# A hybrid decoder trunk on one core: the two merge gates as seven-product blocks, the attention projection behind them, and another order of the block products

## The chip, the cores and the metric

The kernel runs on one core of one Trainium2 chip. The metric is the device time of one execution in microseconds (us), lower is better. Before the change it is 2224.86 us (median of 3 runs, 2223.46 to 2225.05).

## The reference, cut to what matters

Two layers, 512 tokens, width 1024, all in float32. Each layer has a token-mixing sublayer and a SwiGLU sublayer, and the residual stream is normalized after each.

```python
z = einsum('bsd,dc->bsc', x, w_in) + b_in          # one projection, 11648 columns
q_a, k_a, v_a, q_r, k_r, v_r, g_r, gate_a, gate_b = split(z)
y_a = dilated_window_attention(q_a, k_a, v_a)      # 3 groups combined, width 384
y_b = silu(g_r) * group_norm(retention(q_r, k_r, v_r))   # 4 heads, width 2048
merged = sigmoid(gate_a) * (y_a @ w_attn_proj) + sigmoid(gate_b) * (y_b @ w_ret_proj)
x = layer_norm(ALPHA * x + merged @ w_out)
h = silu(x @ w_gate) * (x @ w_up)                  # D_FF = 2816
x = layer_norm(ALPHA * x + h @ w_down)
```

`gate_a` and `gate_b` are the last two pieces of the input projection, 1024 columns each. They read the layer's input `x`, the same for both.

## The kernel before, in words

**Numbers in two parts.** Each float32 operand is held as a high part (rounded to the matmul's float32r format) and a low part, the rest. `hilo` makes them: a copy on ACT for the high part, a subtraction on DVE for the low one. A product takes three matmuls: high x high, high x low, low x high (`mm3`, line 83; all of them appear in the profile as L81). `unit` (line 112) does the same for a tile of weights, which `load` (line 107) brought by a DMA of SP's queue into one of eight buffers of the pool `rawp`. The parts lie in `whi` and `wlo`, four buffers each.

**Tiles.** A tile of PSUM is 128 x 512, and there are eight. The layer's input lies transposed in `xh` and `xl`: 128 partitions by 8 pieces of the width by 512 tokens.

**Plain products.** `wstat` takes 128 columns of weights as the stationary operand and all 512 tokens as the moving one, 8 x 3 matmuls of 512.

**Block products.** Where two halves of the width, two halves of the tokens and two halves of the columns meet, the kernel multiplies 2 x 2 blocks with seven products instead of eight (Winograd's form). The left blocks are A11, A12, A22 (parts of `xh`, `xl`) and four sums S1 to S4 of blocks, which `x_sums` has put into `xs`; the right blocks are weights: B11, B21, B22, and sums P1 to P4. P1 and P3 are made by DMA: SP loads one block and a DMA of POOL's queue adds the second one to it in place (`Right.load`, L314). P2 and P4 are made from P1 in place by a DVE addition (`Right.begin`, L340). `Right.high` makes the high part (L323) and, one step later, the low part (L329); the operands of a product are prepared one product ahead (`Right.operands`). The table `ORDER` says in which order the products go, and `CHAIN` which PSUM tile a product adds to: products 1, 6, 7 and 4 add to tile A, 5 and 3 to tile C, 2 has its own:

```python
ORDER = ((1, "A11", "B11"), (2, "A12", "B21"), (5, "S1", "P1"), (3, "S4", "B22"),
         (6, "S2", "P2"), (7, "S3", "P3"), (4, "A22", "P4"))
CHAIN = {1: "A", 6: "A", 7: "A", 4: "A", 2: "X", 5: "C", 3: "C"}
```

After each product, `ev` reads what the tile holds by then: a copy on ACT after 1, 5 and 6, an addition or subtraction on DVE after 2, 3 and 7, the rest after 4. `wide` (line 390) runs such a block with 256 columns of weights stationary and 256 tokens moving: 7 x 24 matmuls of 256 columns. Before the change only the FFN uses it, in `ffn_pair`: 256 columns of the up matrix and the same 256 of the gate matrix, ten such pairs a layer (in parts of 2, 4 and 4, each followed by its share of the down projection). `tall` is the other form, with tokens stationary; it serves the values and gates of the retention heads (`ret_values_gates`) and the attention's values, and follows `ORDER` too.

**Order of the work.** The text gives an order, and the framework's scheduler then orders the instructions of each engine by its own estimate of what is ready, so that matmuls of a later product can stand ahead of an earlier one. Besides, the kernel keeps a list `side` of small steps (attention blocks, retention scores and outputs, transposes), which `tick` takes one by one between matmuls at a rate that `pace` sets; `drain` runs what is left.

**The stage that changes.** At the end of the mixing sublayer, after the last retention head's values and gates, a loop runs over four passes `dp` of 256 output channels. A pass computes both gates with `wstat` (4 x 24 matmuls of 512), takes the sigmoid (L916), stores gate b to the DRAM tile `g_d` by a DMA of ACT's queue (L918), loads 256 columns of `w_attn_proj`, multiplies them with the attention output `ya` (18 matmuls of 512), multiplies that by gate a (L928) and stores it to `g_d` by a DMA of POOL's queue (L929). In `side` meanwhile: the outputs of head 3 (`ret_outputs(3)`), then the first half of the retention output `y_d`, which is loaded (`y_load`) and split into `xs` (`y_put`), since nobody needs the sums in there any more. The next stage reads `g_d` back, and multiplies `w_ret_proj` with the retention output; it puts the second half of it into `xh` and `xl`.

Of the kernel before, what the change touches and what calls it, by code (L numbers as in the profile page):

```python
# [11 lines left out]
F32 = mybir.dt.float32  # L12
F32R = mybir.dt.float32r
AF = mybir.ActivationFunctionType
ALU = mybir.AluOpType
# [3 lines left out]
P = 128  # L19
S = 512  # L20
D = 1024
KD = D // P
# [4 lines left out]
NG = 3  # L27
# [14 lines left out]
C_GA = C_GR + RH * RV  # L42
C_GB = C_GA + D
# [10 lines left out]
def hybrid_kernel(ctx, tc, x, rel_bias, w_in, b_in, w_attn_proj, w_ret_proj, w_out,  # L54
# [3 lines left out]
    pe, act, dve, pool = nc.tensor, nc.scalar, nc.vector, nc.gpsimd  # L58
# [32 lines left out]
    def hilo(src, hi, lo):  # L91
        act.copy(out=hi, in_=src)  # L92
        dve.tensor_tensor(out=lo, in0=src, in1=hi.bitcast(F32), op=ALU.subtract)  # L93
# [4 lines left out]
    def work(name):  # L98
        return wk.tile([P, S], F32, tag="w2", name=name)
# [7 lines left out]
    def load(src, a, b):  # L107
        v = view(raw(), a, b)
        nc.sync.dma_start(v, src)
        return v  # L110

    def unit(v):
        a, b = v.shape[1], v.shape[2]
        h = view(wp.tile([P, 1024], F32R, tag="whi", name="whi"), a, b)
        l = view(wp.tile([P, 1024], F32R, tag="wlo", name="wlo"), a, b)
        hilo(v, h, l)
        return h, l
# [13 lines left out]
    side, rate, credit, awaited = deque(), [1.0], [0.0], [0] * NI  # L131
# [9 lines left out]
    def pace(us):  # L141
        rate[0], credit[0] = len(side) / us, 0.0

    def drain():
        while side:
            side.popleft()()
# [49 lines left out]
    def pair_units(w, c, c2=None):  # L196

        vs = []
        for hf in range(2):
            ks = slice(4 * hf, 4 * hf + 4)  # L200
            if c2 is None:
                vs.append(load(w[:, ks, c:c + 256], 4, 256))
            else:
                vs.append(view(raw(), 4, 256))
                for q, cc in enumerate((c, c2)):
                    nc.sync.dma_start(vs[hf][:, :, q * P:(q + 1) * P], w[:, ks, cc:cc + P])
        return [unit(v) for v in vs]
# [20 lines left out]
    def wstat(us, q):  # L228

        need(*range(NI))  # L230
        ps = psum("ps")
        for k in range(KD):
            h, l = part_of(us, k, q)
            mm3(ps, h, l, xh[:, k], xl[:, k], k == 0, k == KD - 1)
            tick(STEP)
        return ps
# [41 lines left out]
    def tail_units(raws):  # L278

        out_ = []  # L280
        for j, r in enumerate(raws):
# [12 lines left out]
    ORDER = ((1, "A11", "B11"), (2, "A12", "B21"), (5, "S1", "P1"), (3, "S4", "B22"),  # L294
             (6, "S2", "P2"), (7, "S3", "P3"), (4, "A22", "P4"))
    CHAIN = {1: "A", 6: "A", 7: "A", 4: "A", 2: "X", 5: "C", 3: "C"}
    FIRST = (1, 2, 5)

    class Right:

        def __init__(self, src, shapes):
            self.src, self.shapes, self.t = src, shapes, {}

        def load(self, *names):
            for n in names:
# [24 lines left out]
        def begin(self, n):  # L333

            if n == "B11":
                self.load("B11", "B21", "P1", "P3", "B22")
            elif n in ("P2", "P4"):
                for u in range(len(self.shapes)):
                    r = self.t["P1", u]
                    dve.tensor_tensor(out=r, in0=r, in1=self.t["B22" if n == "P2" else "B21", u], op=ALU.add)  # L340
            return self.high(n)

        def operands(self):

            ahead = self.begin("B11")
            for i in range(len(ORDER)):
                now, low = ahead
                low()
                ahead = self.begin(ORDER[i + 1][2]) if i + 1 < len(ORDER) else None
                yield now  # L350

    def x_left(an, j, ts_):

# [35 lines left out]

    def wide(right, left, ev):  # L390

        ps = {}
        for (i, an, bn), ((h, l),) in zip(ORDER, right.operands()):
            c = CHAIN[i]
            if i in FIRST:
                ps[c] = psum("ps")
            for q in range(2):
                cs = slice(q * P, (q + 1) * P)
                for k in range(4):
                    ah, al = left(an, k, slice(0, 256))  # L400
                    mm3(ps[c][:, q * 256:(q + 1) * 256], h[:, k, cs], l[:, k, cs], ah, al,
                        i in FIRST and q == 0 and k == 0, k == 3)
                    tick(STEP / 2)
            if i != 3:
                ev(i, ps[c])
            if i == 6:
                ev(3, ps["C"])
            yield

    def run(g):  # L410
        for _ in g:
            pass
# [204 lines left out]
    def layer(ly, cp):  # L617
        w_l = rows(w_in[ly])
# [3 lines left out]
        def bcol(c):  # L622
            return bT[:, c // P:c // P + 1]
# [10 lines left out]
        def slot(name="op", dt=F32R):  # L634
            return opp.tile([P, 2, S], dt, tag="op", name=name)
# [179 lines left out]
        with stage("ret") as rp:  # L815
# [64 lines left out]
                side.extend(ret_outputs(h))  # L880


            ya = []
            for t in range(NG):
                o_ = slot("ya")
                hilo(yaT[:, t], o_[:, 0], o_[:, 1])
                ya.append(o_)
            wa_l, wr_l = rows(w_attn_proj[ly]), rows(w_ret_proj[ly])
            y_v = rows(y_d)
            ylow = xs.rearrange("p s h k t -> p (s h k t)").rearrange("p (h k t) -> p h k t", h=2, k=KD)  # L890
# [2 lines left out]
            def y_load(q):  # L893
                yraw[q] = load(y_v[:, 2 * q:2 * q + 2], 2, S)
# [4 lines left out]
            def y_put(q):  # L899
                if q < 4:  # L900
                    hilo(yraw[q], ylow[:, 0, 2 * q:2 * q + 2], ylow[:, 1, 2 * q:2 * q + 2])
                else:
                    ks = slice(2 * q - KD, 2 * q - KD + 2)
                    hilo(yraw[q], xh[:, ks], xl[:, ks])

            for q in range(4):
                side.extend([lambda q=q: y_load(q)] + [nothing] * 4 + [lambda q=q: y_put(q)])
            pace(80)
            for dp in range(KD // 2):
                sg = []  # L910
                for b, c in enumerate((C_GA, C_GB)):
                    us = pair_units(w_l, c + dp * 256)
                    t = slot("sg", F32)
                    for e in range(2):
                        ps = wstat(us, e)
                        act.activation(out=t[:, e], in_=ps, func=AF.Sigmoid, bias=bcol(c + (2 * dp + e) * P))  # L916
                    sg.append(t)
                act.dma_start(g_d[1, dp * 256:(dp + 1) * 256].rearrange("(e p) s -> p e s", p=P), sg[1])  # L918
                h, l = unit(load(wa_l[:, :, dp * 256:(dp + 1) * 256], NG, 256))
                if dp == KD // 2 - 1:  # L920
                    drain()
                for e in range(2):
                    cs = slice(e * P, (e + 1) * P)
                    ps = psum("ps")
                    for t in range(NG):
                        mm3(ps, h[:, t, cs], l[:, t, cs], ya[t][:, 0], ya[t][:, 1], t == 0, t == NG - 1)
                    v = sg[0][:, e]
                    dve.tensor_tensor(out=v, in0=v, in1=ps, op=ALU.mult)  # L928
                pool.dma_start(g_d[0, dp * 256:(dp + 1) * 256].rearrange("(e p) s -> p e s", p=P), sg[0])  # L929
        lay.close()  # L930

        fin = ExitStack()
# [101 lines left out]

        def ffn_pair(f, o_):

            def src(b, u):
                k = 4 if b[1] == "2" else 0
                return (wg_l if b[2] == "2" else wu_l)[:, k:k + 4, f * P:f * P + 256]

            sn = {}

            def put(v, ts_):
                hilo(v, o_[:, 0, :, ts_], o_[:, 1, :, ts_])

            def ev(i, ps):
                p2 = ps.rearrange("p (q t) -> p q t", q=2)
                if i in (1, 5, 6):
                    sn[i] = work("sn").rearrange("p (q t) -> p q t", q=2)
                    act.copy(out=sn[i], in_=p2)  # L1050
                elif i == 2:
                    dve.tensor_tensor(out=sn[1], in0=p2, in1=sn[1], op=ALU.add)
                elif i == 3:
                    v = sn[6]
                    dve.tensor_tensor(out=v, in0=p2, in1=v, op=ALU.subtract)
                    act.activation(out=v, in_=v, func=AF.Silu)
                    dve.tensor_tensor(out=v, in0=v, in1=sn[1], op=ALU.mult)
                    put(v, slice(0, 256))
                elif i == 7:
                    dve.tensor_tensor(out=sn[5], in0=sn[5], in1=p2, op=ALU.subtract)  # L1060
                    act.activation(out=sn[5], in_=sn[5], func=AF.Silu)
                elif i == 4:
                    v = sn[5]
                    dve.tensor_tensor(out=v, in0=v, in1=p2, op=ALU.mult)
                    put(v, slice(256, 512))

            run(wide(Right(src, [(4, 256)]), x_left, ev))

        for part, (f0, f1) in enumerate(FPARTS):
            ht = []  # L1070
# [89 lines left out]
```

## Time and profile before

| | |
|---|---|
| median of 3 runs | 2224.86 us |
| the profiled execution | 2224.68 us |
| its span | 2222.9 us |
| granted TensorE clock | 0.998 |
| PE busy | 2184.1 us (98%), 12330 matmuls |
| DVE busy | 1352.1 us (61%) |
| ACT busy | 946.8 us (43%) |
| POOL busy | 233.5 us (11%) |
| DMA | 325.92 MB, mean 147 GB/s |

The span runs from the first to the last instruction that was profiled. PE is TensorE's matmul, PEld its weight load, DVE the vector engine, ACT the scalar engine, POOL GpSimd, SP the engine that only issues DMAs here; a q behind a name means the engine's queue of DMA issues. In the views, `out<-in` names the tiles that an instruction writes and reads, L81 is line 81 of the kernel, and a bracket at the end of a timeline row tells the idle time of the engine before it and what ended it. A row of a windows view has the window, its length, and the busy time and count of PE, PEld, DVE, ACT and POOL, then the granted clock, the DMA share and GB/s. A row of a group has busy time and mean ns of one, then the idle time before.

### The profile page before, as it was taken

To read this page: it belongs to the slowest core of one execution; us is meant where nothing else is said; L and a number is where in the kernel's file an instruction comes from. 1 tells how busy PE (TensorE), PEld (TensorE's weight loads), DVE (VectorE), ACT (ScalarE), POOL (GpSimd) and SP (SyncE) were. 2 spreads that over 40 slices of the span, in tenths; PEclk is the share of its full clock that TensorE was granted. 3 is DMA by queue.
4 is the path that set the end of the run, shared out by engine and by line. 5 is a ranking of instruction groups with operands and counts; after the bars stand their busy time and mean duration, and the time that the engine had idled before them with its cause. 6 is when DMAs were issued, how large, how long until landed. Compare 5 with 4: busy or idle time off the path is not lost.

```text
span 2222.9 us, 31189 instructions
## 1 busy us (share of the span) xinstructions
PE 2184.1 (98%) x12330; PEld 1884.7 (85%) x12330; DVE 1352.1 (61%) x1971; ACT 946.8 (43%) x1517; POOL 233.5 (11%) x280
## 2 busy tenths in 40 slices
PE   8999999999999999999999999999999999999998
PEld 7877788888888898989898778888888889899896
DVE  5643677875245675646676447777843357666575
ACT  4444544545333253525245445444543234444350
POOL 3110011100000100000040100111000001010001
PEclk9999999999999999999999999999999999999999
DMA  8944266455656356556269343666455562565551
GB/s 226 238 124 103 63 157 170 132 141 157 207 179 190 85 144 141 161 133 152 86 160 243 105 94 85 151 164 157 130 175 192 185 189 64 160 149 155 128 152 38
DMA packets 293300, 325.92 MB, mean 147 GB/s; under 512 B 22478, under 2 KB 231522, under 8 KB 293025
## 3 DMA queue, kind: packets, MB, share of 16 engines
q1 hardware_dynamic: 223488, 244.62, 36.7%
q0 software_dynamic: 42384, 66.52, 15.4%
q10 hardware_dynamic: 27280, 12.80, 2.0%
q8 instruction: 96, 1.57, 0.3%
q14 instruction: 52, 0.42, 0.1%
HBM read 298.09 MB, written 28.53 MB: 147 GB/s over the span
## 4 chain that ended last, share of the span: by engine, by line
PE 80%; issue 10%; DMA 5%; DVE 3%; ACT 2%; POOL 1%; SPq 0%; POOLq 0%; DVEq 0%; ACTq 0%
PE ps L81 72%; PE px L81 6%; DMA raw<-in_w_in 3%; DVE wlo L329 1%; ACT whi L323 1%; PE px L526 1%; PE px L858 1%; DVE wlo L93 0%; POOL ry L124 0%; DMA rb<-in_b_in 0%; PE px L169 0%; DMA exd<-pk 0%; DVE xtok L951 0%; DMA exd<-wb 0%; ACT whi L92 0%
## 5 line engine op out<-in xcount | busy, mean ns | idle before, releaser
L81 PE MATMUL ps<-xh,whi 128*128 128x512 f32 (+1 forms) x1600 | 562.6, 353 | 5.9 <-ACT whi L92 3.3
L81 PE MATMUL ps<-xh,wlo 128*128 128x512 f32 (+1 forms) x1600 | 546.5, 342 | 10.5 <-DVE wlo L329 9.0
L81 PE MATMUL ps<-xl,whi 128*128 128x512 f32 (+1 forms) x1600 | 544.9, 341 | 0.2 <-DVE xl L93 0.2
L329 DVE TENSOR_TENSOR wlo<-raw,whi 128x1024 fp32r<-128x1024 f32 (+1 forms) x308 | 349.4, 1136 | 183.4 <-ACT whi L323 180.3
L323 ACT CAST whi<-raw 128x1024 fp32r<-128x1024 f32 (+1 forms) x308 | 300.4, 979 | 303.1 <-PE ps L81 176.9
L93 DVE TENSOR_TENSOR wlo<-raw,whi 128x1024 fp32r<-128x1024 f32 (+2 forms) x194 | 232.4, 1200 | 300.1 <-ACT whi L92 299.4
L81 PEld LDWEIGHTS ps<-xh,wlo 128*128 128x128 f32 x1600 | 302.7, 189 | 48.8 <-DVE wlo L329 11.5
L81 PEld LDWEIGHTS ps<-xh,whi 128*128 128x128 f32 x1600 | 302.2, 190 | 46.4 <-issue 6.4
L81 PEld LDWEIGHTS ps<-xl,whi 128*128 128x128 f32 x1600 | 303.8, 190 | 29.0 <-DVE xl L93 1.0
L92 ACT CAST whi<-raw 128x1024 fp32r<-128x1024 f32 (+2 forms) x194 | 198.7, 1031 | 285.4 <-PE ps L81 216.5
L81 PE MATMUL ps<-xs,whi 128*128 128x256 f32 (+1 forms) x1536 | 315.1, 302 | 0.0
L81 PEld LDWEIGHTS ps<-xs,whi 128*128 128x128 f32 x1536 | 248.7, 191 | 13.8 <-ACT sn L1050 3.5
L81 PE MATMUL ps<-xs,wlo 128*128 128x256 f32 (+1 forms) x768 | 229.9, 301 | 0.0
L81 PE MATMUL ps<-whi,xs 128*128 128x512 f32 (+1 forms) x768 | 220.0, 360 | 2.8 <-ACT whi L323 1.6
L81 PE MATMUL ps<-whi,ht 128*128 128x512 f32 x576 | 178.8, 390 | 0.0
L81 PEld LDWEIGHTS ps<-whi,xs 128*128 128x128 f32 x768 | 137.7, 188 | 23.6 <-ACT whi L323 2.4
L81 PEld LDWEIGHTS ps<-xs,wlo 128*128 128x128 f32 x768 | 146.5, 191 | 5.4 <-DVE wlo L329 0.4
L81 PE MATMUL ps<-wlo,xs 128*128 128x512 f32 (+1 forms) x384 | 138.3, 360 | 2.7 <-DVE wlo L329 2.5
L81 PEld LDWEIGHTS ps<-whi,ht 128*128 128x128 f32 x576 | 107.4, 188 | 21.4
L314 POOL DMA_DIRECT2D raw<-in_w_ffn_gate x40 | 51.9, 1298 | 675.8 <-DMA raw<-in_w_ffn_up 378.3
L81 PE MATMUL ps<-wlo,ht 128*128 128x512 f32 x288 | 112.8, 392 | 0.3
L81 PE MATMUL ps<-whi,xh 128*128 128x512 f32 (+1 forms) x288 | 103.5, 359 | 1.4 <-DVE sn L453 1.4
(179 smaller groups left out, 2862.3 us busy)
## 6 DMA issues: line engine op xcount, KB each, us to landing
raw<-in_w_in SPq DMA_DIRECT2D x144, 512.0 KB, 4.1
raw<-in_w_ffn_up SPq DMA_DIRECT2D x64, 512.0 KB, 4.5
raw<-in_w_ffn_gate SPq DMA_DIRECT2D x44, 512.0 KB, 3.8
raw<-in_w_ffn_down SPq DMA_DIRECT2D x44, 512.0 KB, 3.7
raw<-in_w_ffn_gate POOLq DMA_DIRECT2D x40, 512.0 KB, 6.4
raw<-in_w_in SPq DMA_DIRECT2D x72, 256.0 KB, 5.0
raw<-in_w_in POOLq DMA_DIRECT2D x32, 512.0 KB, 8.6
raw<-in_w_ret_proj SPq DMA_DIRECT2D x32, 512.0 KB, 4.0
```

The costliest lines, as they stand in the source:

```text
L81: pe.matmul(ps, lhsT=a, rhs=b, start=start, stop=stop, skip_group_check=True)
L92: act.copy(out=hi, in_=src)
L93: dve.tensor_tensor(out=lo, in0=src, in1=hi.bitcast(F32), op=ALU.subtract)
L314: pool.dma_start(r, self.src({"P1": "B12", "P3": "B22"}[n], u), accum_op=ALU.add)
L323: act.copy(out=h, in_=src)
L329: dve.tensor_tensor(out=l, in0=src, in1=h.bitcast(F32), op=ALU.subtract)
L526: pe.transpose(px[:, (2 + j) * P:(3 + j) * P], s[:, hh, j * P:(j + 1) * P], ident)
L858: pe.transpose(px[:, t * P:(t + 1) * P], ys[i][:, t * P:(t + 1) * P], ident)
```

## The change

1. The gates. For each `dp`, 256 columns of gate a and 256 of gate b become the two column halves of one block, and `wide` computes both with seven products of 24 matmuls of 256 (`gates`, with `pair_right`). It uses the sums that are still in `xs`. Gate b gets a tile `sb` of its own (one buffer) in the pool of the retention stage; the four tiles of gate a (`sgs`) are all kept.
2. The attention projection goes into a second loop behind the four gate blocks. `y_put` goes with it, one per pass, since `xs` is now in use until the gates are done; `y_load` 0 and 1 run beside the last gate block, 2 and 3 in the second loop. The splitting of the attention output into `ya` moves from ahead of the gates to beside the last block.
3. The order of products in `wide`, for the gates and for the FFN's pairs, is 1, 5, 6, 2, 7, 3, 4 (`WIDE`); for each layer's first pair (`f == 2`) it is 1, 2, 5, 6, 3, 7, 4 (`WIDE1`). The right blocks are loaded in the order B11, P1, B22, P3, B21. `wide` now calls `ev` after each product, product 3 included. `tall` keeps its order.

```diff
+    WIDE = tuple(ORDER[i] for i in (0, 2, 4, 1, 5, 3, 6))
+    WIDE1 = tuple(ORDER[i] for i in (0, 1, 2, 4, 3, 5, 6))
...
-        def __init__(self, src, shapes):
-            self.src, self.shapes, self.t = src, shapes, {}
+        def __init__(self, src, shapes, order=ORDER, loads=("B11", "B21", "P1", "P3", "B22")):
+            self.src, self.shapes, self.order, self.loads, self.t = src, shapes, order, loads, {}
...
+    def pair_right(w1, w2, c, order=WIDE):
+
+        def src(b, u):
+            k = 4 if b[1] == "2" else 0
+            return (w2 if b[2] == "2" else w1)[:, k:k + 4, c:c + 256]
+
+        return Right(src, [(4, 256)], order, ("B11", "P1", "B22", "P3", "B21"))
...
     def wide(right, left, ev):
...
-        for (i, an, bn), ((h, l),) in zip(ORDER, right.operands()):
+        for (i, an, bn), ((h, l),) in zip(right.order, right.operands()):
...
-            if i != 3:
-                ev(i, ps[c])
-            if i == 6:
-                ev(3, ps["C"])
-            yield
+            ev(i, ps[c])
...
-            ya = []
-            for t in range(NG):
-                o_ = slot("ya")
-                hilo(yaT[:, t], o_[:, 0], o_[:, 1])
-                ya.append(o_)
...
-            for q in range(4):
-                side.extend([lambda q=q: y_load(q)] + [nothing] * 4 + [lambda q=q: y_put(q)])
-            pace(80)
+            def gates(dp, sa, sb):
+
+                sn = {}
+
+                def put(o_, v, c, ts_):
+                    for q in range(2):
+                        act.activation(out=o_[:, q, ts_], in_=v[:, q], func=AF.Sigmoid, bias=bcol(c + (2 * dp + q) * P))
+
+                def ev(i, ps):
+                    p2 = ps.rearrange("p (q t) -> p q t", q=2)
+                    if i in (1, 5, 6):
+                        sn[i] = work("sn").rearrange("p (q t) -> p q t", q=2)
+                        act.copy(out=sn[i], in_=p2)
+                    elif i == 2:
+                        dve.tensor_tensor(out=sn[1], in0=p2, in1=sn[1], op=ALU.add)
+                        put(sa, sn[1], C_GA, slice(0, 256))
+                    elif i == 3:
+                        dve.tensor_tensor(out=sn[6], in0=p2, in1=sn[6], op=ALU.subtract)
+                        put(sb, sn[6], C_GB, slice(0, 256))
+                    elif i == 7:
+                        dve.tensor_tensor(out=sn[5], in0=sn[5], in1=p2, op=ALU.subtract)
+                        put(sb, sn[5], C_GB, slice(256, 512))
+                    elif i == 4:
+                        put(sa, p2, C_GA, slice(256, 512))
+
+                wide(pair_right(w_l[:, :, C_GA:], w_l[:, :, C_GB:], dp * 256), x_left, ev)
+                act.dma_start(g_d[1, dp * 256:(dp + 1) * 256].rearrange("(e p) s -> p e s", p=P), sb)
+
+            pace(40)
...
             for dp in range(KD // 2):
-                sg = []
-                for b, c in enumerate((C_GA, C_GB)):
-                    us = pair_units(w_l, c + dp * 256)
-                    t = slot("sg", F32)
-                    for e in range(2):
-                        ps = wstat(us, e)
-                        act.activation(out=t[:, e], in_=ps, func=AF.Sigmoid, bias=bcol(c + (2 * dp + e) * P))
-                    sg.append(t)
-                act.dma_start(g_d[1, dp * 256:(dp + 1) * 256].rearrange("(e p) s -> p e s", p=P), sg[1])
-                h, l = unit(load(wa_l[:, :, dp * 256:(dp + 1) * 256], NG, 256))
                 if dp == KD // 2 - 1:
                     drain()
+                    side.extend([nothing] * 4 + [lambda t=t: ya_put(t) for t in range(NG)] + [lambda q=q: y_load(q) for q in range(2)])
+                    pace(18)
+                sgs.append(slot("sg", F32))
+                gates(dp, sgs[dp], rp.tile([P, 2, S], F32, tag="sb", name="sb"))
+            drain()
+            was = [unit(load(wa_l[:, :, :256], NG, 256))]
+            for dp in range(KD // 2):
+                h, l = was[dp]
+                y_put(dp)
+                if dp < 2:
+                    y_load(dp + 2)
+                if dp + 1 < KD // 2:
+                    was.append(unit(load(wa_l[:, :, (dp + 1) * 256:(dp + 2) * 256], NG, 256)))
                 for e in range(2):
...
-                    v = sg[0][:, e]
+                    v = sgs[dp][:, e]
...
-            run(wide(Right(src, [(4, 256)]), x_left, ev))
+            wide(pair_right(wu_l, wg_l, f * P, WIDE1 if f == 2 else WIDE), x_left, ev)
```

More of the change, by code (lines that the diff above doesn't have):

```diff
@@ L335, in begin @@
             if n == "B11":
-                self.load("B11", "B21", "P1", "P3", "B22")
+                self.load(*self.loads)
             elif n in ("P2", "P4"):
@@ L345, in operands @@
             ahead = self.begin("B11")
-            for i in range(len(ORDER)):
+            for i in range(len(self.order)):
                 now, low = ahead
                 low()
-                ahead = self.begin(ORDER[i + 1][2]) if i + 1 < len(ORDER) else None
+                ahead = self.begin(self.order[i + 1][2]) if i + 1 < len(self.order) else None
                 yield now
+    def pair_right(w1, w2, c, order=WIDE):
[3 more added lines that the diff above has]
+        return Right(src, [(4, 256)], order, ("B11", "P1", "B22", "P3", "B21"))
     def x_left(an, j, ts_):
@@ L920, in layer, with ya_put @@
+            pace(40)
+            sgs, ya = [], []
+            def ya_put(t):
+                ya.append(slot("ya"))
+                hilo(yaT[:, t], ya[t][:, 0], ya[t][:, 1])
+            for dp in range(KD // 2):
                 if dp == KD // 2 - 1:
                     drain()
+                    side.extend([nothing] * 4 + [lambda t=t: ya_put(t) for t in range(NG)] + [lambda q=q: y_load(q) for q in range(2)])
+                    pace(18)
+                sgs.append(slot("sg", F32))
+                gates(dp, sgs[dp], rp.tile([P, 2, S], F32, tag="sb", name="sb"))
@@ L926, in layer @@
                         mm3(ps, h[:, t, cs], l[:, t, cs], ya[t][:, 0], ya[t][:, 1], t == 0, t == NG - 1)
-                    v = sg[0][:, e]
+                    v = sgs[dp][:, e]
                     dve.tensor_tensor(out=v, in0=v, in1=ps, op=ALU.mult)
-                pool.dma_start(g_d[0, dp * 256:(dp + 1) * 256].rearrange("(e p) s -> p e s", p=P), sg[0])
+                pool.dma_start(g_d[0, dp * 256:(dp + 1) * 256].rearrange("(e p) s -> p e s", p=P), sgs[dp])
         lay.close()
@@ L1035, in ffn_pair @@
         def ffn_pair(f, o_):
-            def src(b, u):
-                k = 4 if b[1] == "2" else 0
-                return (wg_l if b[2] == "2" else wu_l)[:, k:k + 4, f * P:f * P + 256]
             sn = {}
```

## The prediction

> **What bounds the kernel now.** I read the totals first, then windows of the two stages that the change touches, then their matmuls in the timeline, then the waits of PE.
>
> ```profile
> span 2222.9 us, 31189 instructions
> PE 2184.1 (98%) x12330; PEld 1884.7 (85%) x12330; DVE 1352.1 (61%) x1971; ACT 946.8 (43%) x1517; POOL 233.5 (11%) x280
> ```
>
> PE is busy for 98% of the span, so the time is the number of matmuls times the distance between their starts (I call it the pitch), plus the places where PE waits. "Busy" hides small gaps, since the matmuls overlap, so I take pitches from starts. The first window below is one pass `dp` of the old gate loop (layer 0), the next two are one pair of FFN block products each.
>
> ```profile
> 574.23:600.07 25.84, 25.84 (x116) 21.40 (x115) 7.20 (x7) 7.58 (x10) 0.72 (x1) 1.00 0.60 204
> 876.81:898.30 21.49, 20.74 (x171) 20.31 (x170) 15.23 (x16) 10.90 (x14) 2.83 (x3) 1.00 0.72 172
> 898.30:919.80 21.50, 20.75 (x171) 20.32 (x170) 15.14 (x16) 11.00 (x15) 1.28 (x1) 1.00 0.74 180
> ...
> 580.12 0.39 PE L81 MATMUL ps<-xh,wlo 128*128 128x512 f32 x1
> 580.35 0.39 PE L81 MATMUL ps<-xh,whi 128*128 128x512 f32 x1
> ...
> 900.57 0.28 PE L81 MATMUL ps<-xh,whi 128*128 128x256 f32 x1
> 900.69 0.28 PE L81 MATMUL ps<-xl,whi 128*128 128x256 f32 x1
> 900.81 0.28 PE L81 MATMUL ps<-xh,wlo 128*128 128x256 f32 x1
> ```
>
> The granted clock is 1.00 in all three windows. A 512-wide matmul starts every 0.227 us, a 256-wide one every 0.120. A gate pass has 96 gate matmuls and 18 of the projection; 114 x 0.2267 = 25.84, exactly its window: the gate stage has no stall at all, and only fewer matmuls can shorten it. A pair has 7 products x 24 = 168 matmuls; 168 x 0.120 = 20.16, but it takes 21.49: 1.33 us are lost. Where they go:
>
> ```profile
> 895.24 0.29 PE L81 MATMUL ps<-xh,whi 128*128 128x256 f32 x1
> 895.37 0.28 PE L81 MATMUL ps<-xl,whi 128*128 128x256 f32 x1
> 896.41 0.39 PE L81 MATMUL ps<-xh,wlo 128*128 128x256 f32 x1 [0.75 <-DVE wlo L329]
> 896.63 0.28 PE L81 MATMUL ps<-xh,whi 128*128 128x256 f32 x1
> ...
> 897.10 0.40 PE L81 MATMUL ps<-xs,whi 128*128 128x256 f32 x2
> ...
> 900.93 0.37 PE L81 MATMUL ps<-xh,whi 128*128 128x256 f32 x1
> 901.14 0.28 PE L81 MATMUL ps<-xl,whi 128*128 128x256 f32 x1
> 896.32 0.58 ACT L1050 COPY sn<-ps 128x512 f32<-128x512 f32 x1
> PE ps L81 <- DVE wlo L329: 11.6, 16, 1.4
> ```
>
> Product 6 ends near 895.2. Product 7 adds to the same PSUM tile and must wait until ACT has copied that tile (the copy runs 896.32 to 896.90); it starts at 897.10. The gap is filled with 7 matmuls of the next pair's first product, and the third of these waits for its `wlo`: 1.04 instead of 0.12. So 0.92 is lost, 0.10 at the next matmul (0.22), and 0.09 at 900.93, where product 4 waits in the same way for the DVE step behind product 7. That is 1.11 of the 1.33; the remaining 0.22 has another place. The last row, the waits of PE, says that this wait for `wlo` occurs 16 times for 11.6 us in all.
>
> **The change part by part.**
>
> *Gates as block products.* A pass loses 96 matmuls of 0.2267 (21.76) and gets 168 of 0.120 (20.16): 1.60 less. The 18 projection matmuls (4.08) are the same, only later. Eight passes: 8 x 1.60 = 12.8 us. This holds if nothing else falls on the path, so the other engines:
>
> ```profile
> L329 DVE TENSOR_TENSOR wlo<-raw,whi 128x1024 fp32r<-128x1024 f32 x252 | 307.3, 1222 | 159.2 <-ACT whi L323 156.5
> L340 DVE TENSOR_TENSOR raw<-raw 128x1024 f32<-128x1024 f32 x72 | 87.8, 1220 | 1.5
> L323 ACT CAST whi<-raw 128x1024 fp32r<-128x1024 f32 x252 | 262.9, 1047 | 256.4 <-PE ps L81 151.1 <-issue 76.0 <-ACT whi L323 11.4
> L1050 ACT COPY sn<-ps 128x512 f32<-128x512 f32 x60 | 34.8, 581 | 3.9 <-PE ps L81 3.9
> L916 ACT ACTIVATE sg<-ps,bT 128x512 f32<-128x512 f32 x32 | 22.0, 686 | 43.9 <-PE ps L81 42.8 <-PE px L81 1.1
> L852 DVE SCALAR_TENSOR_TENSOR yb<-px,mv,gs 128x512 f32<-128x512 f32 x32 | 23.7, 741 | 0.0
> L848 DVE BATCH_NORM_STATS2 st<-px 128x6 f32<-128x512 f32 x32 | 22.2, 694 | 9.2 <-PE px L81 9.2
> L928 DVE TENSOR_TENSOR sg<-sg,ps x16: 678/686/689, 545.6 to 1723.2; 128x512 f32<-128x512 f32 x16
> ```
>
> DVE per gate block: 7 `wlo` of 1.22, 2 adds of 1.22, 3 PSUM steps near 0.69: 13.1 us of 20.2. ACT: 7 casts of 1.05, 3 copies of 0.58, 8 sigmoids of 256 columns, each between half of 0.69 and 0.69 (I take 0.45): 12.7 of 20.2. Neither is the bound. In the first two blocks head 3's outputs still run beside: four times 0.69 + 0.74 = 5.7 us and small DVE steps besides, over some 40 us, which brings DVE to (26.2 + 5.7)/40.3 = 79% and more. At the pair's 15.2 of 21.5 (71%) PE waits only where a PSUM tile held it first; nearer to full it may wait elsewhere. I charge 0.5 us per layer, between 0 and 3.
>
> *The projection behind the gates.* Four passes of 4.08 us now stand together, 16.3 us. On DVE each has `y_put` 1.22, the low half of `wa` (768 of 1024 columns, so about 0.92) and two multiplies of 0.69: 3.52 of 4.08. The `y_put` that the gates hid before is now here, and right behind it the next stage wants its first two weight units (2 x 1.22) before PE can run it. In the old order that spare time was plentiful. The cost if the cover is gone is what DVE is late, between 0 and the two units plus one `y_put`, 3.7 us a layer; 0.5 is my value, since 16.3 - 14.1 = 2.2 us are free for 2.4 of work. On ACT the 4 x (1.05 + 0.8) of casts leave half of it free. The `wa` loads, `y_load` 2 and 3, stand in SP's queue behind the third block's loads and need buffers of `rawp` (8); PE's last gate products (2.9 us each) cover a cast of 1.05 + 1.22. `g_d[0]` is written by POOL in the projection instead of along the gates; its first reader is 16 us further on, its last 40.
>
> *One buffer `sb`.* The block's ACT may write it only when the block before has been stored. The store is issued at the end of a block; the first new write follows product 7, the fifth of seven, 14.4 us later.
>
> ```profile
> g_d<-sg ACTq DMA_DIRECT2D x8, 512.0 KB, 5.5
> raw<-in_w_in POOLq DMA_DIRECT2D x32, 512.0 KB, 8.6
> raw<-in_w_ffn_gate POOLq DMA_DIRECT2D x40, 512.0 KB, 6.4
> raw<-in_w_ffn_gate SPq DMA_DIRECT2D x44, 512.0 KB, 3.8
> L314 POOL DMA_DIRECT2D raw<-in_w_ffn_gate x40: 1273/1292/1387, 722.1 to 2126.5; - x40
> ```
>
> It lands in 5.5, so this costs nothing; if it were late, ACT would hold the next `whi` casts behind the sigmoid.
>
> *The order of products.* With 1, 5, 6, 2, 7, 3, 4 every reuse of a PSUM tile has another product (2.88 us) in between: 1 and 6 have 5, 6 and 7 have 2, 7 and 4 have 3. The copy (0.58) and the DVE step (0.69) fit in that. So 1.11 goes in the pairs that are followed by another pair: 14 of 20 (10 pairs a layer in parts of 2, 4, 4; the last of each part is followed by the down projection), 15.5 us. In the other six the gap is filled by down-projection matmuls and loses less:
>
> ```profile
> 938.24 1.10 PE L81 MATMUL ps<-whi,ht 128*128 128x512 f32 x4
> 939.40 0.50 PE L81 MATMUL ps<-wlo,ht 128*128 128x512 f32 x1
> 939.74 0.40 PE L81 MATMUL ps<-whi,ht 128*128 128x512 f32 x1
> ```
>
> Four matmuls in 1.16 instead of 0.91, and 0.34 instead of 0.23: 0.36 each, 2.2 in all. Together 17.7.
>
> What is late next: P1 now stands second. It needs its load, POOL's accumulating DMA, cast and low half, and P2 is made from it in place directly after. These rows show how far ahead they run now:
>
> ```profile
> 874.89 10.63 SPq L109 DMA_DIRECT2D raw<-in_w_ffn_gate  x2
> 875.79 1.29 POOL L314 DMA_DIRECT2D raw<-in_w_ffn_gate  x1 [21.50 <-DMA raw<-in_w_ffn_up]
> 887.59 1.22 DVE L340 TENSOR_TENSOR raw<-raw 128x1024 f32<-128x1024 f32 x1
> 902.63 1.22 DVE L340 TENSOR_TENSOR raw<-raw 128x1024 f32<-128x1024 f32 x1
> 907.85 0.40 PE L81 MATMUL ps<-xs,whi 128*128 128x256 f32 x2
> ```
>
> The second load of that SP row (B22) is issued as the stretch ends, at 874.89 + 10.63 = 885.5, and is not there when the add at 887.59 begins, 2.1 us later (landings of 512 KB take 3.8 in the median here); so it feeds the add at 902.63, in the pair whose product 1 began at 895.24. Its accumulation was issued at 875.79, so P1 as second product (from about 898) would leave 22 us, less 6.4 to land, less 1.05 + 1.22: 13 us spare. For the first gate block the queue is shared with head 3's small POOL steps, and with ten raw tiles a block in the stage before the loads run less far ahead; 8.6 to land still fits in the 16 us of that stage's last three products. I take 0.
>
> **The sum.** The profiled execution took 2224.68 (span 2222.9 and 1.78 around it); the median of the runs is 2224.86. 2224.7 - 12.8 - 17.7 + 2 x (0.5 + 0.5) = 2196.2.
>
> The Trainium skill, "TensorE: Matmul & The Clock Gate", section "Back-to-back issue gap", gives N/2.4 + 2.5 ns for a warm isolated gap, 215.8 and 109.2 ns. By it the eight passes would gain 8 x (96 x 0.2158 - 168 x 0.1092) = 19.0 us, an estimate, and the time would be 6 lower. The trace disagrees on both widths, 0.227 and 0.120, and the measured pitches decide.
>
> **The rivals.**
>
> *A. The stall moves and stays.* The order of the instructions on PE is not the order of the text (7 matmuls of the next pair ran early). A new order may leave another gap of the same size, for instance at the seam from the last product to the next pair. For it: it is the filler that stalled, not product 7 itself. Against it: without a gap there is nothing to fill. Then the FFN gains nothing: 2224.7 - 12.8 + 2 = 2214.
>
> *B. The gates starve.* The fuller DVE and the tight projection eat the 1.60 of each pass: 2224.7 - 17.7 = 2207. For it: 1.6 us of 20 is little. Against it: FFN pairs with more DVE work lose only to the PSUM tile.
>
> *C. Slower: the chain P1 to P2.* Low half of P1, add, cast, low half of P2: 1.22 + 1.22 + 1.05 + 1.22 = 4.71 us; and with P1 and P2 neighbours only product 5 (2.88) lies between if P1's low half is made no earlier than product 5 starts. That is 1.83 a block; 28 blocks, 51 us: 2196 + 51 = 2247. It decides from 28.5/28 = 1.02 us a block. Against it: four `whi` and four `wlo` buffers let casts run up to three products ahead: the add for P2 at 902.63 comes before even the product ahead of it starts (907.85).
>
> *D. Slower: P1's second half arrives late.* DVE is busier, and POOL writes 16 accumulating DMAs more. Only a landing over 19 us (13 spare and 6.4) would stall PE; a landing of 22 at each of 28 blocks costs 84 us: 2280. Against it: 40 such issues took 1.27 to 1.39 us of POOL's time with DVE 71% busy.
> The rule that speaks for it is in the Trainium skill, "SBUF — State Buffer", "SBUF: two separate sides": descriptors of a DMA issued by POOL cannot be written while DVE holds the shared port. These issues vary by 0.11 us, so the trace shows no such hold here.
>
> **How the numbers follow.** Forecast 0.64; A 0.13, B 0.12, C 0.05, D 0.02, the change doing nothing that can be told 0.04. The prediction is the forecast's 2196. Low end: both charges 0 and the remaining 0.22 x 20 gone too, 2190, and 4 us for the width of what the rows don't show: 2186. High end takes in B and A: 2214. That leaves out C, D, no change, and a little of each side, some 0.17. What a measurement tells from no change is 0.2%, 4.4 us: faster is forecast, A and B, 0.89; same 0.04; slower 0.07.
>
> **What would show it.** A block in the gates and an FFN pair should each take 20.2 to 20.5 us; PE's waits for `wlo` should fall from 11.6 to under 3; four projection passes should stand in 16.3 to 17.5 us. It is wrong if pairs still take 21.4 (A), if gate blocks take over 21.5 (B), if PE waits for `whi` or `wlo` at the third product (C) or at the second with POOL just before it (D).

## The result, and the profile after

The changed kernel takes 2187.89 us (median of four runs, 2186.94 to 2194.89) against 2224.24 before: ratio 0.9843, 95% interval 0.9823 to 0.9864. It is 36.4 us faster; 28.5 were forecast, and the time lies near the lower end of the range. The profiled execution took 2188.09.

The head of the page of the changed kernel, and its waits of PE:

```profile
span 2186.3 us, 32588 instructions
PE 2160.0 (99%) x12906; PEld 1900.6 (87%) x12906; DVE 1412.5 (65%) x2035; ACT 988.1 (45%) x1597; POOL 254.1 (12%) x296
...
PE ps L81 <- ACT whi L92: 3.3, 1, 3.3
PE px L533 <- ACT s L525: 2.5, 2, 1.3
...
PE ps L81 <- DVE wlo L331: 1.2, 3, 0.4
```

There are more matmuls than before (12906 recorded against 12330), in less time. L331 is the old L329: the wait for `wlo` has gone from 11.6 us to 1.2. Of the others, only one of 0.2 us in each layer (for `xh`, in the FFN) lies in the stages that the change touches.

To see where the time went, I cut each layer at two starts that both kernels have: from the last high part of a retention value (ACT, `vr`) to the first matmul of `w_out` (this holds the gates, the projection and the next stage), and from the last matmul of `w_out` to the last of the down projection (the FFN). The windows of before, layer 0 and layer 1, then those of after:

```profile
514.05:712.95 198.90, 198.90 (x887) 164.73 (x886) 87.12 (x110) 71.44 (x84) 7.01 (x11) 1.00 0.57 187
757.65:1117.82 360.17, 354.52 (x2433) 328.08 (x2432) 229.21 (x263) 148.42 (x188) 30.42 (x25) 1.00 0.51 131
1610.82:1809.72 198.90, 198.90 (x887) 164.73 (x885) 87.29 (x110) 71.44 (x84) 7.01 (x11) 1.00 0.56 186
1854.43:2213.18 358.75, 353.10 (x2422) 326.91 (x2420) 227.93 (x263) 145.09 (x182) 29.18 (x23) 1.00 0.49 125
```

```profile
510.65:703.06 192.41, 192.41 (x1175) 173.37 (x1173) 116.52 (x141) 92.10 (x124) 13.53 (x16) 1.00 0.73 221
747.76:1096.75 348.99, 348.75 (x2434) 327.20 (x2432) 228.95 (x263) 148.38 (x188) 30.35 (x25) 1.00 0.53 135
1592.26:1784.67 192.41, 192.41 (x1174) 173.36 (x1173) 116.41 (x141) 91.89 (x124) 13.53 (x16) 1.00 0.73 221
1829.37:2176.94 347.57, 347.33 (x2421) 326.03 (x2420) 227.41 (x263) 145.34 (x182) 29.14 (x23) 1.00 0.51 129
```

The gate stage gives 6.49 us a layer, 12.98 in all: PE has no idle time in it before or after, and DVE's work rises from 87 to 117 us of its window without being seen. The FFN gives 11.18 a layer, 22.36 in all, with the same matmuls; its idle time of PE falls from 5.65 to 0.24 (the rest of the gain does not show as idle time: a matmul of 256 lasts 0.28 us and the next starts after 0.12, so the first 0.16 us of each gap count as busy). Together 35.3. The rest of the 36.4 lies outside these windows, most of it in the attention stages, which the change leaves alone: the time to the start of the first window is 508.6 to 514.1 in the twelve profiles of this study, and 510.1 to 514.1 in the five whose kernels are the same up to there (before, e5, e6, e8, e10). So a single profile is good to some 3 us as a whole. The gate window repeats to 0.01 us, and the FFN window to 0.3. Below I use them.

A gate block and an FFN pair in the changed kernel (two stretches in the gates, chosen by length; ACT's silu of successive pairs):

```profile
540.20:560.40 20.20, 20.20 (x172) 20.20 (x171) 14.82 (x19) 13.27 (x22) 3.12 (x3) 1.00 0.77 202
560.40:580.60 20.20, 20.20 (x172) 20.20 (x171) 13.15 (x14) 12.59 (x21) 0.06 (x1) 1.00 0.67 184
...
866.31 0.63 ACT L1089 ACTIVATE sn<-sn 128x512 f32<-128x512 f32 x1
886.47 0.63 ACT L1089 ACTIVATE sn<-sn 128x512 f32<-128x512 f32 x1
906.63 0.63 ACT L1089 ACTIVATE sn<-sn 128x512 f32<-128x512 f32 x1
```

Pairs come every 20.16 us: 168 x 0.120, nothing lost. The two stretches show that PE is busy throughout in the gates, not where a block begins. By the starts of its matmuls the last gate block of each layer takes 20.16 us too, and the four projection passes behind it take 16.35.

### The profile page after: what moved, and what is told of

The parts are those of the page before. It is cut to its first block, busy times and chain, and to the rows that moved or that the text cites. A ratio compares the mean times of both kernels' runs of the same rounds, so it can differ in the third digit from the quotient of the medians.

```text
span 2186.3 us, 32588 instructions
## 1 busy us (share of the span) xinstructions
PE 2160.0 (99%) x12906; PEld 1900.6 (87%) x12906; DVE 1412.5 (65%) x2035; ACT 988.1 (45%) x1597; POOL 254.1 (12%) x296
## 4 chain that ended last, share of the span: by engine, by line
PE 82%; issue 9%; DMA 3%; DVE 3%; ACT 1%; POOL 1%; POOLq 0%; DVEq 0%; ACTq 0%; SPq 0%
PE ps L81 75%; PE px L81 5%; DMA raw<-in_w_in 2%; PE px L865 1%; PE px L533 1%; POOL ry L124 0%; DMA exd<-wb 0%; DVE wlo L331 0%; PE px L169 0%; DMA exd<-pk 0%; DVE wlo L93 0%; DVE xtok L988 0%; DMA mb<-exd 0%; DMA rb<-in_b_in 0%; ACT whi L92 0%
## 5 line engine op out<-in xcount | busy, mean ns | idle before, releaser
L331 DVE TENSOR_TENSOR wlo<-raw,whi 128x1024 fp32r<-128x1024 f32 (+1 forms) x364 | 418.1, 1150 | 210.0 <-ACT whi L325 207.3
L81 PE MATMUL ps<-xh,whi 128*128 128x256 f32 (+1 forms) x1536 | 515.7, 337 | 4.4 <-ACT whi L92 3.3
L325 ACT CAST whi<-raw 128x1024 fp32r<-128x1024 f32 (+1 forms) x364 | 358.8, 990 | 342.1 <-PE ps L81 198.5
L81 PE MATMUL ps<-xh,wlo 128*128 128x256 f32 (+1 forms) x1536 | 500.5, 327 | 1.1 <-DVE wlo L93 0.9
L81 PE MATMUL ps<-xl,whi 128*128 128x256 f32 (+1 forms) x1536 | 500.5, 326 | 0.2 <-DVE xl L93 0.2
L81 PE MATMUL ps<-xs,whi 128*128 128x256 f32 (+1 forms) x2048 | 404.6, 296 | 0.0
L81 PEld LDWEIGHTS ps<-xs,whi 128*128 128x128 f32 x2048 | 327.8, 191 | 10.3
L81 PE MATMUL ps<-xs,wlo 128*128 128x256 f32 (+1 forms) x1024 | 303.4, 296 | 0.0
L316 POOL DMA_DIRECT2D raw<-in_w_in x64 | 80.3, 1273 | 358.2 <-DMA raw<-in_w_in 160.8
L342 DVE TENSOR_TENSOR raw<-raw 128x1024 f32<-128x1024 f32 (+1 forms) x104 | 119.5, 1149 | 2.1
```

The source lines that it names most:

```text
L81: pe.matmul(ps, lhsT=a, rhs=b, start=start, stop=stop, skip_group_check=True)
L316: pool.dma_start(r, self.src({"P1": "B12", "P3": "B22"}[n], u), accum_op=ALU.add)
L325: act.copy(out=h, in_=src)
L331: dve.tensor_tensor(out=l, in0=src, in1=h.bitcast(F32), op=ALU.subtract)
```

## The experiments

Each ratio is to runs of the kernel before on the same chip; the last two columns are the two windows of layer 0, in us.

| kernel | median us | ratio (95%) | gate stage | FFN |
|---|---|---|---|---|
| before | 2224.24 | | 198.89 | 360.17 |
| changed | 2187.89 | 0.9843 (0.9823 to 0.9864) | 192.41 | 348.99 |
| e1, order alone | 2200.83 | 0.9899 (0.9882 to 0.9917) | 198.89 | 348.99 |
| e2, gates alone | 2213.23 | 0.9953 (0.9938 to 0.9968) | 192.41 | 360.45 |
| e3, old order everywhere | 2215.34 | 0.9960 (0.9946 to 0.9975) | 194.07 | 360.16 |
| e4, old loads | 2188.62 | 0.9844 (0.9826 to 0.9862) | 192.41 | 349.00 |
| e5, no wait 6 to 7 | 2207.80 | 0.9931 (0.9914 to 0.9947) | 198.89 | 353.57 |
| e6, no wait at all three | 2200.74 | 0.9900 (0.9885 to 0.9915) | 198.89 | 348.86 |
| e7, order 1 5 3 6 2 7 4 | 2207.24 | 0.9929 (0.9913 to 0.9945) | 198.47 | 351.95 |
| e8, 256-wide plain gates | 2231.29 | 1.0037 (1.0025 to 1.0049) | 204.00 | 360.12 |
| e9, projection inside | 2188.90 | 0.9843 (0.9828 to 0.9858) | 192.47 | 348.99 |
| e10, no wait 5 to 3 | 2209.14 | 0.9945 (0.9928 to 0.9961) | 198.89 | 353.89 |

**The two halves apart: e1 and e2.** e1 is the kernel before with the new order of products and loads in the FFN alone. e2 is the changed kernel with

```diff
-            wide(pair_right(wu_l, wg_l, f * P, WIDE1 if f == 2 else WIDE), x_left, ev)
+            wide(pair_right(wu_l, wg_l, f * P, ORDER, ("B11", "B21", "P1", "P3", "B22")), x_left, ev)
```

and `wide` holds the step after 3 back until 6 is done, as before.

> The new order of products (and of their loads) in the FFN's pairs alone; gates, projection and y_put as before. Theory (PE's stalls in a pair are three reuses of a PSUM tile that is still being read: 6 to 7, 7 to 4 and 5 to 3, together 1.33 us a pair): the FFN part of each layer falls by 11.2 us as in the changed kernel, 22.4 in all, 2224.2 - 22.4 = 2201.8. As the prediction summed it (1.11 of the 1.33 only, 17.7): 2206.5. Rival (the changed gates also help the FFN, by what they leave in the queues): over 2206.5.

> The gates as block products in the new order with the projection behind them; the FFN's pairs keep the old order and the old order of loads. Theory (only the count of matmuls matters, 8 x 1.60 us): 2224.2 - 12.8 = 2211.4, pairs still 21.5 us. Rival (each pass gives part of it back at the seams to the projection and to the next stage, 2 us as the prediction charged, or all of it as in rival B): 2213.4 to 2224.

e1 took 2200.83, within 1 us of the theory that counts all three stalls, and not 2206.5. The FFN window of e1 is that of the changed kernel, and the gate window of e2 too: the halves do not touch each other. The median of e2 alone, 2213.2, would fit the rival as well; the gate window, 192.41 without idle PE, says that nothing is lost at the seams and that the 1.8 us above the theory lie elsewhere.

**Is it the order of loads? e4.**

```diff
-        return Right(src, [(4, 256)], order, ("B11", "P1", "B22", "P3", "B21"))
+        return Right(src, [(4, 256)], order, ("B11", "B21", "P1", "P3", "B22"))
```

> The changed kernel, but the blocks are loaded in the old order B11, B21, P1, P3, B22 (products in the new order). Theory (loads run a block ahead, some 13 us spare for P1): no difference, 2188 within 2 us. Rival (the new order of products works only because P1 is loaded second; P1's accumulation, 6.4 to 8.6 us to land, is late otherwise): 28 blocks by 0.5 us or more, 2202 or more.

No difference, so the place of P1 among the loads does not matter. That P1 and P2 as second and third product cost nothing (rivals C and D) is shown by the changed kernel itself: its pairs take 20.16 us.

**Are the waits for `wlo` made by the reuse of PSUM? e5 and e6.** Both are the kernel before with one argument changed in `wide`:

```diff
             if i != 3:
-                ev(i, ps[c])
+                ev(i, ps["X" if i in (6,) else c])        # e6: (5, 6, 7)
```

> The kernel before, with one thing changed in wide: the copy after product 6 reads product 2's PSUM tile instead of tile A, so that product 7 need not wait for it (this part of the result is then left out). Same instructions, same old order of products. Theory (the wait for wlo is a consequence: matmuls of the next pair were put into the gap that this reuse makes, and they are the ones that wait): no gap, no early matmuls; 0.92 + 0.10 us in 14 pairs and 0.36 in 6 go, 2224.2 - 16.4 = 2208, and PE's waits for wlo fall from 11.6 us to under 3. Rival (DVE is simply late with wlo): 2224, the waits stay.

> As the one before, and the readers after products 5 and 7 read product 2's tile too, so that 5 to 3 and 7 to 4 are free of waits as well (these parts of the result are left out). Theory: the remaining 0.09 and 0.22 us of a pair go too, a pair takes 20.16 us and the time is that of the new order alone, 2201.8. Rival (the 0.22 is something else, for instance a pause of PE's instruction supply at that place): 2206.

In both, PE's wait for `wlo` all but goes: from 11.6 us to 0.8 in e5 and 1.2 in e6. The times came out to 0.2 us (e5, 2207.8 for 2208) and 1.1 us (e6, 2200.7 for 2201.8), but for e5 that is partly luck: its FFN windows gain 6.6 us a layer, 13.2 in all and not 16.4. A pair of e5 still takes 20.63, since with 6 to 7 free the loss between 7 and 4 grows from 0.09 to 0.25 us. With all three waits gone, the old order runs as fast as the new one: 348.86 and 348.99 us of FFN. So the new order's whole gain is that no product meets a PSUM tile that is still being read.

**Do the gates suffer the same stalls in the old order? e3.** e2, and the gates with `ORDER` and the old loads too.

> Gates as block products and the projection behind them, but the old order of products and of loads everywhere, in the gates too. Theory: each gate block then has the pair's three stalls, 1.33 us, against 1.60 gained by fewer matmuls; eight blocks keep 8 x 0.27 = 2.2, so 2222, a gate block takes 21.5 us. Rival (the stalls belong to the FFN, with its longer chain of silu, product and high/low parts, and the gates have none): 2211.4.

A miss, nearer to the rival: the old order costs the gates 1.66 us a layer, 0.41 a block on average instead of 1.33, although the gaps are there. This is the gap after product 6 in a gate block of e3, filled as in the FFN with matmuls of the next block (`xh`, `xl`):

```profile
576.28 0.28 PE L81 MATMUL ps<-xs,wlo 128*128 128x256 f32 x1
576.40 0.28 PE L81 MATMUL ps<-xh,whi 128*128 128x256 f32 x1
576.52 0.28 PE L81 MATMUL ps<-xl,whi 128*128 128x256 f32 x1
576.68 0.39 PE L81 MATMUL ps<-xh,wlo 128*128 128x256 f32 x1
```

The first matmul with `wlo` starts after 0.16, not 1.04: here the matmuls that fill the gap (the filler) have their operands ready, and the gap costs next to nothing. So the gap after 6 alone could not be the cause of the 0.92 in the FFN. The filler's operands were late there, and I looked for why. These are the rows before the change, in the FFN (PE around the gap between 5 and 3, then ACT and DVE), and below them ACT in the gate block of e3:

```profile
889.24 0.40 PE L81 MATMUL ps<-xs,whi 128*128 128x256 f32 x2
...
890.68 0.77 PE L81 MATMUL ps<-xs,whi 128*128 128x256 f32 x3
891.29 0.28 PE L81 MATMUL ps<-xs,wlo 128*128 128x256 f32 x1
...
893.80 0.28 PE L81 MATMUL ps<-xs,wlo 128*128 128x256 f32 x1
893.92 0.28 PE L81 MATMUL ps<-xs,whi 128*128 128x256 f32 x1
894.04 0.28 PE L81 MATMUL ps<-xs,wlo 128*128 128x256 f32 x1
...
889.36 1.05 ACT L323 CAST whi<-raw 128x1024 fp32r<-128x1024 f32 x1 [1.83 <-PE ps L81]
890.31 0.58 ACT L1050 COPY sn<-ps 128x512 f32<-128x512 f32 x1
894.05 1.05 ACT L323 CAST whi<-raw 128x1024 fp32r<-128x1024 f32 x1 [3.15 <-issue]
895.13 2.54 DVE L329 TENSOR_TENSOR wlo<-raw,whi 128x1024 fp32r<-128x1024 f32 x2 [3.46 <-ACT whi L323]
...
570.62 0.59 ACT L924 COPY sn<-ps 128x512 f32<-128x512 f32 x1 [1.12 <-PE ps L81]
574.32 1.05 ACT L325 CAST whi<-raw 128x1024 fp32r<-128x1024 f32 x1 [1.34 <-PE ps L81]
```

Product 6 follows product 5 here from 889.24, ahead of product 3, which waits for the copy of tile C. The copy stands behind a cast on ACT (889.36) and ends only at 890.89; PE has a small hole before 890.95, and then product 3 starts. Thirteen matmuls of product 6 are drawn forward, from 889.24 to 890.68: a step of a product is two matmuls with `whi` and one with `wlo`, and the step that the hole cuts in two after its first matmul is completed at 893.92 and 894.04, right behind product 3. So product 3's last matmul starts at 893.80, 1.8 us later than if product 3 had followed product 5 directly. At 894.05 ACT begins the cast that the filler needs. So the chain theory: the first gap delays product 3, product 3 holds a `whi` buffer that the cast is waiting for, and the filler of the second gap comes up short. In e3's gate block ACT makes the copy without a cast ahead of it, only six matmuls come ahead of product 3, and the cast begins at 574.32, 2.1 us ahead of the filler instead of 1.2.

**The chain tested: e10.** The edit of e5 with `i == 5`: 6 to 7 and 7 to 4 stay as they were.

> The kernel before, with only the copy after product 5 reading product 2's tile instead of tile C (this part of the result is left out), so that product 3 need not wait for it; 6 to 7 and 7 to 4 stay neighbours as they were. Chain theory, formed on the runs so far: the gap between 5 and 3 was filled with 12 matmuls of product 6, product 3 therefore ended 1.44 us later, its whi buffer came free later, and the cast for the matmuls that fill the gap after 6 began too late, which is why these waited for wlo. Then this one edit takes away most of the 0.92 us as well: pairs of 20.3 to 20.6, the FFN part 360.17 falls to about 350 to 352, 2204 to 2207. Rival (three separate stalls, as the prediction counted them): only the 0.25 goes, FFN 357.7, 2219.

(The expectation counts 12 drawn-forward matmuls and 1.44 us; the rows above make it 13, and 1.8 with the hole.) The windows of two successive pairs of e10, its gap after product 6, and the cast that the filler needs:

```profile
870.55:891.02 20.47, 20.47 (x170) 20.25 (x169) 15.23 (x17) 10.95 (x15) 2.58 (x2) 1.00 0.71 166
891.02:911.49 20.47, 20.47 (x171) 20.25 (x169) 15.23 (x17) 11.00 (x15) 2.56 (x2) 1.00 0.77 189
...
889.70 0.28 PE L81 MATMUL ps<-xl,whi 128*128 128x256 f32 x1
889.82 0.28 PE L81 MATMUL ps<-xh,wlo 128*128 128x256 f32 x1
...
891.02 0.28 PE L81 MATMUL ps<-xh,whi 128*128 128x256 f32 x1
891.29 0.39 PE L81 MATMUL ps<-xs,whi 128*128 128x256 f32 x1
...
886.83 1.05 ACT L323 CAST whi<-raw 128x1024 fp32r<-128x1024 f32 x1 [0.42 <-PE ps L81]
```

Pairs fall from 21.49 to 20.47, within the chain's 20.3 to 20.6; the rival gives 21.24. The gap after 6 is still there, now filled with 13 matmuls that do not wait at all: the cast for them begins 2.8 us ahead. The FFN's 353.89 is above the 350 to 352 that I expected (by the starts of the matmuls, the layer's first pair still loses some 1.3 us and its last 1.1), and the median of 2209.1 above 2204 to 2207 with it, but far from 357.7. Taking away the first gap (6.3 us a layer) or the second (6.6) each takes the 0.92 out of a pair that another pair follows; both together, with 7 to 4, give 11.3. That the `whi` buffer carries the delay is shown by the semaphore records of the three traces. The cast for the next pair's B11 is the fourth after that of product 3's operand B22, and `whi` has four buffers. In each kernel ACT's queue waits ahead of that cast until the last matmul of product 3 that reads `whi` is done: it starts at 893.68 before the change, 574.00 in e3 and 886.46 in e10, and the cast 0.32 to 0.37 us later. (The row of 894.05 says `issue`, since that wait stands in a semaphore instruction of its own, which the view leaves out.) No run gives `whi` a fifth buffer or puts the copy ahead of the cast on ACT, so what either would gain is open.

**Neighbours without the big stall: e7.**

```diff
-    WIDE = tuple(ORDER[i] for i in (0, 2, 4, 1, 5, 3, 6))
+    WIDE = tuple(ORDER[i] for i in (0, 2, 3, 4, 1, 5, 6))
```

with the step after 3 held back as in e2. In the FFN that step then multiplies by the up half without product 2's part.

> The changed kernel with the products in the order 1, 5, 3, 6, 2, 7, 4 in gates and FFN (each layer's first pair as changed; the step after product 3 waits for product 6, as before the change). Here 6 and 7 have product 2 between them, but 5 and 3 are neighbours again and so are 7 and 4. Theory (each neighbourhood costs its own stall, 0.22 and 0.09 us): 26 blocks by 0.31, 2188 + 8 = 2196. Rival (only 6 to 7 matters, because the gap after it is filled with early matmuls): 2188. Other rival (a gap of any kind is filled with matmuls whose wlo is late): 2188 + 26 x 1.1 = 2217.

The FFN behaves as the theory said: a pair takes 20.46, and 351.95 is 2.96 above the changed kernel, 0.3 a pair. The gates do not: 198.47 in layer 0 and 199.50 in layer 1, 6 and 7 us more than the changed kernel's, most of it in one place of each layer's first block. With that the whole, 2207.24, misses the forecast of 2196 by 11 us. PE, DVE and POOL at that place in layer 0:

```profile
537.62 0.39 PE L81 MATMUL ps<-xh,whi 128*128 128x256 f32 x1 [3.14 <-DVE sn L932]
...
536.36 0.22 DVE L125 SCALAR_TENSOR_TENSOR rt<-ry,ve 128x1 f32<-128x1 f32 x1 [3.26 <-POOL ry L124]
536.88 0.68 DVE L932 TENSOR_TENSOR sn<-sn,ps 128x512 f32<-128x512 f32 x1
...
524.49 1.31 POOL L316 DMA_DIRECT2D raw<-in_w_in  x1 [2.72 <-ACT whi L325]
534.45 1.28 POOL L316 DMA_DIRECT2D raw<-in_w_in  x1 [8.65 <-DMA raw<-in_w_in]
535.23 1.10 POOL L124 TENSOR_TENSOR ry<-ve,mhalf 128x1 f32<-128x1 f32 x1
```

Read from below: POOL's queue waits 8.65 us for a load before it can issue an accumulating DMA; behind it stands a power of one column for head 3's group norm; DVE waits for that; behind it on DVE stands the step after product 7; and product 4 waits for that. The same wait is in the changed kernel (DVE):

```profile
535.92 0.22 DVE L125 SCALAR_TENSOR_TENSOR rt<-ry,ve 128x1 f32<-128x1 f32 x1 [2.92 <-POOL ry L124]
536.06 0.68 DVE L925 TENSOR_TENSOR sn<-ps,sn 128x512 f32<-128x512 f32 x1
```

There the step that is held up is the one after product 3, on a tile that no later product adds to, and PE does not notice. This is the queue that the prediction named and priced at 0.

**The price of narrow matmuls: e8.** The kernel before; `wstat` for the gates runs tokens 0 to 255 and then 256 to 511.

```diff
+        for t in range(2):
+            ts_ = slice(t * 256, (t + 1) * 256)
+            for k in range(KD):
+                h, l = part_of(us, k, q)
+                mm3(ps[:, ts_], h, l, xh[:, k, ts_], xl[:, k, ts_], k == 0, k == KD - 1)
```

> The kernel before, with the gates' plain products done 256 tokens at a time: 192 matmuls of 256 a pass instead of 96 of 512, nothing else. Theory (0.120 us against half of 0.2267, 0.0067 more for each, so block products give back 1.12 us of each pass, and would gain 2.7 instead of 1.60 at the wide pitch): 8 x 192 x 0.0067 = 10.2 us slower, 2234.4. Rival (the weight load, twice as many of them at 0.19 us, shows as more than the pitch when the two halves use the same weights far apart): over 2240.

The gate stage grows by 5.11 and 5.08 us in the two layers, 10.2 in all, as worked out; the median rose by 8.1 to 2231.3, and the difference lies outside the gate windows. An eighth fewer products would be worth 2.7 us a pass; 1.1 of it goes to the narrower matmul.

**The seams: e9.** The loop of the projection is inside the gate passes again, `ya` is made ahead of them, and the four `y_put` follow the last gate block.

> The changed kernel with the projection back inside each gate pass and the attention output split ahead of the gates, as before the change; the four y_put then stand together after the last gate block instead of one per projection pass. It tests the charge of 1 us a layer at the seams and the cover of y_put. Theory (matmuls alone count while DVE's work is spread; here 4 x 1.22 us of y_put and the first weight units, 2.4, meet in the last projection pass of 4.1 us, so some 3.2 us are late in each layer): 2188 + 6 = 2194, and the stretch from the last retention values to w_out 195.6 instead of 192.41. Rival (y_put has cover even so, since the next stage reads it piece by piece over 10 us): 2188, 192.4.

The rival: 192.47, without idle PE. Even four `y_put` in one place are covered; that the reason is the next stage's reading piece by piece is the rival's argument and not tested by itself. Where the projection stands makes no difference here.

## Why the prediction was right, step by step

- *The gates, 12.8 us:* measured 12.98, and e8 confirms the pitch under it. The measured pitches, and not the formula of the Trainium skill's page "TensorE: Matmul & The Clock Gate", section "Back-to-back issue gap" (19.0), gave the gain.
- *The seams and DVE's fullness, 2 us:* mis-sized; measured 0 (the gate windows of the changed kernel, e2 and e9 have no idle PE). DVE's work in the gate stage rose by 29 us a layer, and all of it stayed beside PE. Rival B is out.
- *The order, 17.7 us:* the step that was mis-sized most; measured 22.36. The 0.22 us a pair that "has another place" was the third reuse, between 5 and 3 on tile C, which I had not looked at: the list of reuses named 1 to 6, 6 to 7 and 7 to 4 and left out that one. 20 x 0.22 = 4.4 is nearly all of the 4.7 between the two. That the new order separates 5 and 3 as well is luck, as far as the prediction goes: it does not name that reuse.
- *Its mechanism* was right that the reuse is the cause (e6) and that a product in between removes it, but wrong in counting the stalls one by one: the 0.92 needs both gaps (e5 and e10), and in the gates the same order cost 0.41 a block, not 1.33 (e3). The prediction put it down to the gap after product 6 alone; it did not see that a `whi` buffer ties the filler to product 3.
- *P1 in second place, 0:* right (pairs of 20.16 us; the order of loads makes no difference, e4). *POOL's shared queue, 0:* right in the time, though a wait is there and e7 shows what hides it. *Rival A* is out: pairs take 20.16.
- *The sum:* 28.5 forecast, plus 0.2 for the gates, 2.0 for the seams and 4.7 for the order, makes some 35.3, as in the windows; the other 1.0 lies outside them. All three terms erred to the same side, so the time came out 8.3 us below the forecast, inside the range only by the 4 us kept at its low end.

## What to carry to other kernels

When products add to few PSUM tiles and something reads a tile between them, list every reuse of every tile and put another product into each. It needs no further buffer here. A gap that the scheduler fills is free only if the filler's operands are ready, so look at what the row after the gap waits for, and then at what held that operand's buffer. Two stalls that share a buffer are not a sum: take one away alone and see what is left of the other. Price a trade of wide for narrow matmuls by the starts of both widths in the trace: here the narrow ones took back 1.1 of the 2.7 us that a pass would have gained.

## What the runs showed of the hardware

In the first gate block of e7 PE idled for 3.14 us and then ran thirteen matmuls at the granted clock of 1.00. After that it slowed down (windows before the stall, after it, and later; then the two slow stretches alone, in layer 0 and layer 1):

```profile
520.00:534.00 14.00, 13.98 (x109) 13.53 (x109) 9.87 (x18) 7.98 (x12) 1.86 (x2) 1.00 0.67 165
539.10:542.60 3.50, 3.50 (x19) 3.50 (x19) 1.23 (x1) 1.04 (x3) 0.00 (x0) 0.51 0.75 222
543.00:557.00 14.00, 14.00 (x109) 13.51 (x108) 8.22 (x13) 7.13 (x10) 0.55 (x1) 1.00 0.38 112
539.17:542.58 3.41, 3.41 (x19) 3.41 (x18) 1.23 (x1) 0.95 (x3) 0.00 (x0) 0.50 0.74 222
1628.02:1631.43 3.41, 3.04 (x14) 3.04 (x15) 1.49 (x2) 2.21 (x4) 0.00 (x0) 0.50 1.16 253
...
539.33 0.41 PE L81 MATMUL ps<-xl,whi 128*128 128x256 f32 x1
539.54 0.41 PE L81 MATMUL ps<-xh,wlo 128*128 128x256 f32 x1
```

The granted clock was 0.50 for 3.41 us, and a matmul started every 0.213 us instead of 0.120, which adds some 1.5 us to the stall. The slow stretch began 1.5 us after PE was busy again in layer 0; in layer 1, where PE idled for 4.31 us, it began 0.4 us before PE was busy again. The Trainium skill, "TensorE: Matmul & The Clock Gate", section "What's actually happening", says that the gate judges PE by windows of 3.4 us that run on regardless of the kernel; the length agrees with these rows, and so does the half clock; the two slow stretches begin 1088.85 us apart, which is 319 times 3.413. PE's 3.14 us without work is shorter than one such stretch, and yet the clock fell.
